# The beginning of a two-layer trunk kernel: conditioning row by rounded and low diagonals, the first modulation sum in two halves, the identity on another queue, the lower bound moved back

## The chip, the cores and the metric

The kernel runs on one core of one Trainium2 chip. The metric is device time in microseconds of one execution, as the median of several runs. Engines are named as in the profile: PE (TensorE's matmuls), PEld (its weight loads), DVE (VectorE), ACT (ScalarE), POOL (GpSimd), and SP, which here only issues transfers.

## The reference, cut to what matters

Two layers work on 512 positions of 1024 channels. The first mixes by a gated linear recurrence, the second by chunked band attention, and each has a SwiGLU feed-forward part. In front of each part stands an RMS norm whose result is scaled and shifted by a vector computed from one conditioning vector `c`:

```python
c_act = jax.nn.silu(c)
sm = jax.nn.softmax(a_lb, axis=0)
lower_bounds = jnp.cumsum(sm, axis=0) - sm[0]
...
mod = c_act @ mod_w[layer] + mod_b[layer]
sh1, sc1, g1, sh2, sc2, g2 = jnp.split(mod, N_MOD, axis=-1)
u = modulate(rms_norm(h, norm_mix[layer]), sh1, sc1)     # x * (1 + scale) + shift
# first mixer:
q, z_f, v, g = jnp.split(u @ w_in, [...], axis=-1)
f = lbf + (1 - lbf) * jax.nn.sigmoid(z_f)
```

There is one layer of the first kind, so the softmax for the lower bound runs over one element, and the bound is zero.

## The kernel before, in words

Data lie with channels on the 128 partitions: `h[j]`, j = 0 to 7, is 128 channels by 512 positions. Weights and activations are each split into a rounded high part (by ACT) and the remainder as a low part (by DVE), and a product is three matmuls: high by high, high by low, low by high (`mm3`).

*The opening.* SP issues the loads. `cols` (all the small vectors by columns) comes first, then `ident` (a 128x128 identity), then, for each j, a row block of the modulation matrix (`mrow`, 512 KB), `h[j]` (256 KB) and the first weights (`first_r`, six blocks of 128 columns, 384 KB). ACT takes the sigmoid of `c`, DVE multiplies it by `c` to get `cact`. DVE then scales the identity by one column of `cact` at a time (`dc`, L1293), and PE multiplies a matrix of ones by each of these diagonals (L1294): every partition of `crow` then holds the whole row of 1024 conditioning values. ACT and DVE copy it from PSUM to SBUF (L1306 to L1308). `KEEP` matmuls whose result is not used (L1305) keep PE at work meanwhile.

*The loop over j.* `mod_entry(j, 1)` (L952, L955) multiplies a block of the modulation matrix by `crow` on DVE and adds along the row; ACT makes the scale `a1[j]` from it. `rounded` (L974, ACT) and `rest` (L977, DVE) give the two parts of `h[j]` times that scale; `high` (L962, ACT) and `low` (L965, DVE) the two parts of the first weights; `square` (ACT) and an addition (L1322, DVE) the squares for the norm. `first_mm(j)` is 18 matmuls into six PSUM banks, the projections of heads 0 to 2 before the norm's factor and shift. When the squares of all j are added, `mean_square` (L295) and, after ACT and POOL, `bcast` (L313, L314) give the norm's factor on all partitions; the products of j = 6 stand around them, and those of j = 7 after.

*After that* the normed `u` is made, the value projection (`av`) begins, `shift_sums` on DVE and L1404 on PE give the biases `fb`, and `gates(0, None)` (L1021 to L1044) takes the sigmoids of heads 0 and 1. The lower bound enters there, as `lb` and `oml` (one minus it).

*Order.* From the loads to `push(56)` the code stands in `tc.manual_schedule()`: its instructions keep the order in which they are written, on each engine. Instructions outside that block are placed by the compiler's list scheduler, before, between or after them. The lower bound and `cact` stand outside it in the kernel before. The heads' recurrence (`core`, whose DVE lines L1059 and L1068 alternate with PE's L1078 and L1092) and the remaining projections (`filler`, advanced by `push`) follow outside the block.

Of the kernel before, what the change touches and what calls it, by code (L numbers as in the profile page):

```python
# [62 lines left out]
V1_AFTER, CREDIT, RATES = 1, 3.0, (3.5, 16, 1.375, 56, 1.5)  # L63


KEEP = 5


EARLY = (3, 5)
# [6 lines left out]
def trunk(ctx: ExitStack, tc: tile.TileContext, d, out):  # L76
# [13 lines left out]
    cols = cst.tile([P, NCOL], F32, tag="cols", name="cols")  # L90
    nc.sync.dma_start(cols, d["cols"])
    ident = cst.tile([P, P], F32, tag="ident", name="ident")
    nc.sync.dma_start(ident, d["ident"])
    h = [cst.tile([P, S], F32, tag=f"h{j}", name=f"h{j}") for j in range(KT)]

    ones = cst.tile([P, P], F32, tag="ones", name="ones")
# [9 lines left out]

    lb = cst.tile([P, AH], F32, tag="lb", name="lb")
    oml = cst.tile([P, AH], F32, tag="oml", name="oml")
    lbt = sm.tile([P, AH], F32, tag="lbt", name="lbt")
    V.tensor_sub(lbt, cols[:, C_LB:C_LB + AH], cols[:, C_LB:C_LB + AH])  # L110
    lbe = sm.tile([P, AH], F32, tag="lbe", name="lbe")
    A.activation(lbe, lbt, AF.Exp)
    lbr = sm.tile([P, AH], F32, tag="lbr", name="lbr")
    V.reciprocal(lbr, lbe)
    lbs = sm.tile([P, AH], F32, tag="lbs", name="lbs")
    V.tensor_mul(lbs, lbe, lbr)
    V.tensor_sub(lb, lbs, lbs)
    V.tensor_scalar(oml, lb, -1.0, 1.0, op0=ALU.mult, op1=ALU.add)

    cact = cst.tile([P, KT], F32, tag="cact", name="cact")  # L120
    csig = sm.tile([P, KT], F32, tag="csig", name="csig")
    A.activation(csig, cols[:, C_C:C_C + KT], AF.Sigmoid)
    V.tensor_mul(cact, cols[:, C_C:C_C + KT], csig)


    def by_transfer(key):
# [800 lines left out]
    def load_mod(j, v):  # L927

        if v and j in (0, 2):
            t = hp.tile([P, 3, D], F32, tag="kq", name=f"mrow{v}_{j}", bufs=2)  # L930
            for i, k in enumerate((j, 4 + j, 5 + j)):
                mrow[k, 1] = t[:, i, :]
        elif v and j < 4:
            mrow[j, v] = hp.tile([P, D], F32, tag="f", name=f"mrow{v}_{j}", bufs=2)
        elif not v and j in (4, 5):
            if j == 4:
                t = hp.tile([P, NB, D], F32, tag="vt", name="mrow0_4")
                mrow[4, 0], mrow[5, 0] = t[:, 0, :], t[:, 1, :]
        elif not v:
            pool, tag = ((hp, "mraw2"), (mp, "mraw"))[j in (2, 3)]  # L940
            mrow[j, v] = pool.tile([P, D], F32, tag=tag, name=f"mrow{v}_{j}", bufs=2)
        nc.sync.dma_start(mrow[j, v], d["modw"][v, j])

    def load_first(j):
        tag = ("on0", "on1", "on2", "a256", "fr4", "fr5", "fr6", "on3")[j]
        fraw[j] = hp.tile([P, 6, P], F32, tag=tag, name=f"first_r{j}")
        nc.sync.dma_start(fraw[j], d["a_first"][j])
# [12 lines left out]
    def high(j):  # L960
        wfs[j] = [wp.tile([P, 6, P], F32R, tag="w" + x, name=f"first{j}_{x}") for x in "hl"]
        A.activation(wfs[j][0], fraw[j], AF.Copy)  # L962

    def low(j):
        V.tensor_sub(wfs[j][1], fraw[j], wfs[j][0])  # L965
# [6 lines left out]
    def rounded(j):  # L972
        u[j] = [up.tile([P, S], F32R, tag=f"u{x}{j}", name=f"u00{x}{j}", bufs=1) for x in "hl"]
        A.activation(u[j][0], h[j], AF.Copy, scale=a1[j])  # L974
# [308 lines left out]
                step()  # L1283

    with tc.manual_schedule():
        dcs = hp.tile([P, KT, P], F32, tag="on3", name="dc")

        pcs = []
        for r in range(2):
            dc = dcs[:, NB * r:NB * r + NB, :]  # L1290
            pcs.append(bank(f"crow{r}"))
            for k in range(NB):
                V.tensor_scalar_mul(dc[:, k, :], ident, cact[:, NB * r + k:NB * r + k + 1])  # L1293
                T.matmul(pcs[r][:, k * P:(k + 1) * P], ones, dc[:, k, :], start=True, stop=True)  # L1294
        for j in range(KT):
            load_mod(j, 1) if (j, 1) not in mrow else nc.sync.dma_start(mrow[j, 1], d["modw"][1, j])
            nc.sync.dma_start(h[j], d["xT"][j * P:(j + 1) * P, :])
            load_first(j)
        for k in range(6):
            load_mod(k, 0)  # L1300
        load(1)
        gb = cst.tile([P, KT], F32, tag="gb", name="gb")
        V.scalar_tensor_tensor(gb, cols[:, C_MB + 8:C_MB + 16], 1.0, cols[:, C_NM:C_NM + KT], op0=ALU.add, op1=ALU.mult)
        for _ in range(KEEP):
            T.matmul(first[0][:, 0:256], ones, dcs[:, 0:2, :].rearrange("p k c -> p (k c)"), start=True, stop=True)  # L1305
        A.activation(crow[:, 0:S], pcs[0], AF.Copy)  # L1306
        A.activation(crow[:, S:S + 256], pcs[1][:, 0:256], AF.Copy)
        V.tensor_copy(crow[:, S + 256:D], pcs[1][:, 256:S])  # L1308
        high(0)
        a1.append(mod_entry(0, 1))  # L1310
        rounded(0)
        square(0)
        for j in range(KT):
            if j == 0:
                low(j)
                rest(j)
            if j + 1 < KT:
                a1.append(mod_entry(j + 1, 1))
            if j:
                rest(j)  # L1320
                low(j)
                V.tensor_add(acc, acc, sqs.pop(j))  # L1322
                if j == KT - 1:
                    pst = mean_square(acc, "n0")
                    rs = rstd(pst, "n0")
                    shs = [mod_entry(0, 0), mod_entry(1, 0)]
                    first_mm(j - 1, range(3))
                    rb = bcast(rs, "n0")
                    first_mm(j - 1, range(3, 6))
                else:  # L1330
                    first_mm(j - 1)
            if j + 1 < KT:
                rounded(j + 1)
                high(j + 1)
                square(j + 1)
        rbs = hp.tile([P, S], F32, tag="rbs", name="rbs")
        A.activation(rbs, rb, AF.Copy)
        shs.append(mod_entry(2, 0))
        ts = []

        def weighted(k):
            if k < KT:
                ts.append(normed(k, a1[k]))

        def complete(k):

            def between():
                if 1 < k < KT - 1:
                    shs.append(mod_entry(k + 1, 0))
                if k != 1:  # L1350
                    weighted(k + 1)

            shifted(k, ts[k], shs[k], between)
            if k == 1:
                weighted(2)
            if k < 2:
                load_mod(6 + k, 0)

        state["meanwhile"] = lambda: (weighted(0), complete(0))
        fetch(0, 0)  # L1360
        first_mm(KT - 1)
        early = {p: (hp.tile([P, 3, 2, S], F32, tag="kq", name=f"kq{p}", bufs=2),
                     hp.tile([P, 2, S], F32, tag="f", name=f"f{p}", bufs=2)) for p in range(2)}

        def evacuate(i):
            hd = i // 2
            A.activation(early[hd // 2][1][:, hd % 2, :] if i % 2 == 0 else early[hd // 2][0][:, 0, hd % 2, :],
                         first[i], AF.Copy)

        pa = hp.tile([P, 6, P], F32, tag="ad", name="first_pa")  # L1370

        def shift_sums(k):

            if k:
                V.scalar_tensor_tensor(pa, fraw[k], shs[k], pa, op0=ALU.mult, op1=ALU.add)
            else:
                V.tensor_scalar_mul(pa, fraw[0], shs[0])

        def renorm(i):

            hd = i // 2
            t = early[hd // 2][1][:, hd % 2, :] if i % 2 == 0 else early[hd // 2][0][:, 0, hd % 2, :]
            V.tensor_mul(t, first[i] if hd else t, rbs)

        complete(1)
        for kp in range(KT // 2):
            if kp + 1 < KT // 2:
                state["meanwhile"] = lambda: complete(2 * kp + 2)
            push(8 * kp + 1)
            if kp == 0:  # L1390
                evacuate(0)
                evacuate(1)
            if kp + 1 < KT // 2:
                complete(2 * kp + 3)
            push(8 * kp + 8)
        for k in range(KT):
            shift_sums(k)
            if k > 4:
                push(33 + 6 * (k - 5))
        for i in range(4):  # L1400
            renorm(i)
        pb = bank("first_b")
        for i in range(6):
            T.matmul(pb[:, i:i + 1], pa[:, i, :], ones[:, 0:1], start=True, stop=True)  # L1404
        fb = cst.tile([P, 2, 6], F32, tag="fb", name="fb")
        V.tensor_copy(fb[:, 0, :], pb[:, 0:6])
        state["mods_after"] = V.tensor_scalar_mul(fb[:, 1, :], pb[:, 0:6], -1.0)
        fetch(state["used"], SPLIT_AHEAD)
        gate[0] = gates(0, None)
        renorm(4)  # L1410
        renorm(5)
        u = [u[j] for j in range(KT)]
        push(56)
# [540 lines left out]
```

## Time and profile before

| | |
|---|---|
| median of 3 runs | 1214.94 us (1214.26 to 1215.57) |
| profiled execution, its own time | 1215.52 us |
| its span, first to last instruction | 1213.6 us |
| PE busy | 1199.2 us |
| DVE busy | 1008.5 us |
| ACT busy | 670.4 us |
| mean granted TensorE clock | 0.999 |

The span is 1.9 us shorter than the execution's time, because the time includes what lies before the first and behind the last instruction. A row of a timeline has the start in us from the span's start, the duration, the engine (with a q for its queue's own instructions), the source line, the operation, the tile written and those read, the shapes, the count, and in brackets the idle time of the engine before it with what ended it. A row of the chain has start, length and what was running or being waited for. In a group's row, the numbers behind the bar are busy time and the mean ns of one, and then the engine's idle time before them.

### The profile page before, as it was taken

The numbers are of one execution on the slowest core, as the hardware profiler recorded it, in microseconds if no ns is written. First come the engines' busy times: TensorE is split into PE (matmuls) and PEld (weight loads), VectorE is DVE, ScalarE is ACT, GpSimd is POOL, SyncE is SP. The second block draws the span as 40 slices with busy tenths as digits, with TensorE's granted clock in tenths as the row PEclk, the third lists the DMA queues.
The fourth block names the chain that finished last, engine by engine and source line by source line (L and its number), as shares of the span: only waits on it lengthen the run. The fifth ranks groups of instructions, "written<-read, shape, count | busy, mean of one in ns | idle before, by whom it ended". The sixth has DMA issues, their size and how long they took to land.

```text
span 1213.6 us, 22300 instructions
## 1 busy us (share of the span) xinstructions
PE 1199.2 (99%) x8758; PEld 1052.1 (87%) x8758; DVE 1008.5 (83%) x1821; ACT 670.4 (55%) x1204; POOL 51.0 (4%) x59
## 2 busy tenths in 40 slices
PE   8999999999999999999999999999999999999997
PEld 7887788788899999988888887777889999998997
DVE  8997778778989999987688878886797888977984
ACT  6455456443656666652228556674465566666553
POOL 0100000000000000000001100000100000001100
PEclk9999999999999999999999999999999999999999
DMA  9643354365423444458776987783734566546842
GB/s 356 255 128 104 106 191 141 108 204 191 121 89 125 154 140 140 138 191 280 235 238 180 251 236 201 195 251 79 214 98 157 184 202 207 171 133 153 221 125 92
DMA packets 71401, 211.94 MB, mean 175 GB/s; under 512 B 7552, under 2 KB 10240, under 8 KB 71296
## 3 DMA queue, kind: packets, MB, share of 16 engines
q1 hardware_dynamic: 63952, 194.27, 48.3%
q0 software_dynamic: 7200, 15.99, 7.8%
q8 instruction: 68, 1.11, 0.4%
q14 instruction: 37, 0.30, 0.1%
q10 hardware_dynamic: 144, 0.26, 0.1%
HBM read 204.99 MB, written 20.97 MB: 186 GB/s over the span
## 4 chain that ended last, share of the span: by engine, by line
PE 85%; DVE 7%; ACT 2%; issue 2%; DMA 2%; SPq 0%; POOL 0%; POOLq 0%; ACTq 0%; DVEq 0%
PE f_r L644 9%; PE f_r L645 9%; PE f_r L643 9%; PE f_o L244 4%; PE f_o L243 4%; PE f_o L245 4%; PE f_or L835 2%; PE f_or L834 2%; PE f_or L833 2%; PE bo L1611 1%; PE av L266 1%; PE f L245 1%; PE f L243 1%; PE bo L243 1%; PE f L244 1%
## 5 line engine op out<-in xcount | busy, mean ns | idle before, releaser
L645 PE MATMUL f_r<-f_h,f_w_l 128*128 128x256 f32 x1008 | 278.7, 276 | 0.0
L644 PE MATMUL f_r<-f_l,f_w_h 128*128 128x256 f32 x1008 | 278.7, 276 | 0.0
L643 PE MATMUL f_r<-f_h,f_w_h 128*128 128x256 f32 x1008 | 278.7, 276 | 0.0
L644 PEld LDWEIGHTS f_r<-f_l,f_w_h 128*128 128x128 f32 x1008 | 189.5, 188 | 0.1
L643 PEld LDWEIGHTS f_r<-f_h,f_w_h 128*128 128x128 f32 x1008 | 189.3, 188 | 0.1
L645 PEld LDWEIGHTS f_r<-f_h,f_w_l 128*128 128x128 f32 x1008 | 189.3, 188 | 0.0
L393 DVE SCALAR_TENSOR_TENSOR mw<-mw,crow 128x1024 f32<-128x1024 f32 x96 | 115.7, 1219 | 2.0 <-DMA mw<-in_modw 2.0
L593 ACT ACTIVATE f_w_h<-f_x 128x1024 fp32r<-128x1024 f32 x72 | 76.8, 1066 | 50.4 <-PE f_r L644 38.9
L594 DVE TENSOR_TENSOR f_w_l<-f_x,f_w_h 128x1024 fp32r<-128x1024 f32 x72 | 88.2, 1225 | 8.7 <-ACT f_w_h L593 5.2
L594 DVE TENSOR_TENSOR f_w_l<-r_f_c,f_w_h 128x1024 fp32r<-128x1024 f32 x72 | 68.8, 955 | 21.8 <-ACT f_w_h L593 21.8
L593 ACT ACTIVATE f_w_h<-r_f_c 128x1024 fp32r<-128x1024 f32 x72 | 61.1, 849 | 46.6 <-PE f_r L644 46.6
L149 ACT ACTIVATE f_o_h<-r_f_o 128x1024 fp32r<-128x1024 f32 (+2 forms) x39 | 34.3, 890 | 70.4 <-PE f_o L244 51.5
L244 PE MATMUL f_o<-f_p,f_o_h 128*128 128x512 f32 x176 | 68.6, 390 | 0.0
L245 PE MATMUL f_o<-f_p,f_o_l 128*128 128x512 f32 x176 | 68.5, 390 | 0.0
L243 PE MATMUL f_o<-f_p,f_o_h 128*128 128x512 f32 x176 | 68.3, 389 | 0.0
L1586 ACT ACTIVATE sb<-sb,st 128x128 f32<-128x128 f32 (+1 forms) x64 | 35.8, 559 | 39.3 <-DVE st L1585 39.0
L157 DVE TENSOR_TENSOR f_o_l<-r_f_o,f_o_h 128x1024 fp32r<-128x1024 f32 (+2 forms) x35 | 36.1, 1035 | 22.4 <-ACT f_o_h L149 22.1
L1068 DVE TENSOR_TENSOR kq<-kq,t 128x1024 f32<-128x1024 f32 x28 | 34.2, 1222 | 8.0 <-PE l L1135 3.3
L245 PEld LDWEIGHTS f_o<-f_p,f_o_l 128*128 128x128 f32 x176 | 33.0, 188 | 7.4 <-DVE f_o_l L157 0.5
L244 PEld LDWEIGHTS f_o<-f_p,f_o_h 128*128 128x128 f32 x176 | 33.0, 188 | 7.0 <-DVE f_p L545 0.3
L243 PEld LDWEIGHTS f_o<-f_p,f_o_h 128*128 128x128 f32 x176 | 33.0, 188 | 6.8
L245 PE MATMUL f<-f_h,f_l 128*128 128x512 f32 x96 | 36.9, 391 | 0.3 <-DMA f_l<-r_f 0.3
(517 smaller groups left out, 3213.6 us busy)
## 6 DMA issues: line engine op xcount, KB each, us to landing
mw<-in_modw SPq DMA_DIRECT2D x96, 512.0 KB, 4.5
r_f_c<-in_ffn_in SPq DMA_DIRECT2D x72, 512.0 KB, 3.4
ws<-in_ffn_in SPq DMA_DIRECT2D x18, 512.0 KB, 5.5
ws<-in_ffn_in POOLq DMA_DIRECT2D x18, 512.0 KB, 8.9
f_x<-ws SPq DMA_DIRECT2D x36, 256.0 KB, 3.0
mrow<-in_modw SPq DMA_DIRECT2D x16, 512.0 KB, 8.3
r_f<-in_ffn_in SPq DMA_DIRECT2D x16, 512.0 KB, 3.6
r_f_o<-in_ffn_out SPq DMA_DIRECT2D x16, 512.0 KB, 3.6
```

Source lines behind the costliest of these rows:

```text
L149: A.activation(wh, raw, AF.Copy)
L157: low = V.tensor_sub(wl, raw, wh)
L243: T.matmul(ps, wh[:, kt, :], uh, start=start, stop=False)
L244: T.matmul(ps, wh[:, kt, :], ul, start=False, stop=False)
L245: return T.matmul(ps, wl[:, kt, :], uh, start=False, stop=stop)
L393: V.scalar_tensor_tensor(mw, mw, 1.0, crow, op0=ALU.mult, op1=ALU.mult, accum_out=raw[:, j:j + 1])
L593: A.activation(wh, raw, AF.Copy)
L594: V.tensor_sub(wl, raw, wh)
L643: T.matmul(ps, wh[:, j, :], uh, start=f, stop=False, skip_group_check=True)
L644: T.matmul(ps, wh[:, j, :], ul, start=False, stop=False, skip_group_check=True)
L645: T.matmul(ps, wl[:, j, :], uh, start=False, stop=stop and j == 3, skip_group_check=True)
L1586: A.activation(s[:, 0:n], s[:, 0:n], AF.Exp, bias=st[:, 1:2], accum_out=st[:, 2:3])
```

## The change

- The identity's transfer is issued by ACT instead of SP.
- `cact` is one Silu on ACT instead of a sigmoid on ACT and a product on DVE.
- The lower bound's six small operations become a function, called inside the hand-ordered block between a weight's split and `gates(0, None)`.
- The diagonals are split: ACT writes the rounded diagonal (`dch`), DVE the remainder (`dcl`). PE multiplies ones by four diagonals at a time, once for the rounded and once for the low part, 512 columns each, instead of eight matmuls of 128 columns in full precision. The remainders lie in buffers that the first weights of j = 5 and 6 use later.
- Seven matmuls that only keep PE at work stand ahead of these and eight behind, each ones by ones (128 columns), instead of five of 256 columns.
- For j = 0 the modulation sum is taken in two halves straight from PSUM, each with its own scale step on ACT, and the first weights' parts in two halves. ACT copies all of `crow`.
- In the loop, a j's steps stand together: `high`, `mod_entry`, `rounded`, `square`, `low`, `rest`, addition. Before, the modulation sum of j + 1 stood ahead of `rest` and `low` of j. The products, one j behind, keep their places, and so do `mean_square` and `bcast`.
- Loads of a j come in the order `mrow`, `first_r`, `h`.

```diff
-KEEP = 5
+KEEP = (7, 8)
...
-    nc.sync.dma_start(ident, d["ident"])
+    A.dma_start(ident, d["ident"])
...
+    def lower_bound():
+        V.tensor_sub(lbt, cols[:, C_LB:C_LB + AH], cols[:, C_LB:C_LB + AH])
+        A.activation(lbe, lbt, AF.Exp)
+        V.reciprocal(lbr, lbe)
+        V.tensor_mul(lbs, lbe, lbr)
+        V.tensor_sub(lb, lbs, lbs)
+        V.tensor_scalar(oml, lb, -1.0, 1.0, op0=ALU.mult, op1=ALU.add)
...
-    A.activation(csig, cols[:, C_C:C_C + KT], AF.Sigmoid)
-    V.tensor_mul(cact, cols[:, C_C:C_C + KT], csig)
+    A.activation(cact, cols[:, C_C:C_C + KT], AF.Silu)
...
-        dcs = hp.tile([P, KT, P], F32, tag="on3", name="dc")
-
+        for _ in range(KEEP[0]):
+            T.matmul(first[0][:, 0:P], ones, ones, start=True, stop=True)
+        load_mod(0, 1)
+        load_first(0)
+        nc.sync.dma_start(h[0], d["xT"][0:P, :])
+        dhs = hp.tile([P, KT, P], F32R, tag="on3", name="dch")
+        dls = [hp.tile([P, NB, P], F32R, tag=tag, name=f"dcl_{tag}") for tag in ("fr5", "fr6")]
         pcs = []
         for r in range(2):
-            dc = dcs[:, NB * r:NB * r + NB, :]
             pcs.append(bank(f"crow{r}"))
             for k in range(NB):
-                V.tensor_scalar_mul(dc[:, k, :], ident, cact[:, NB * r + k:NB * r + k + 1])
-                T.matmul(pcs[r][:, k * P:(k + 1) * P], ones, dc[:, k, :], start=True, stop=True)
-        for j in range(KT):
+                c1 = cact[:, NB * r + k:NB * r + k + 1]
+                A.activation(dhs[:, NB * r + k, :], ident, AF.Copy, scale=c1)
+                V.scalar_tensor_tensor(dls[r][:, k, :], ident, c1, dhs[:, NB * r + k, :], op0=ALU.mult, op1=ALU.subtract)
+            for i, x in enumerate((dhs[:, NB * r:NB * r + NB, :], dls[r])):
+                T.matmul(pcs[r], ones[:, :].bitcast(F32R), x.rearrange("p k c -> p (k c)"), start=not i, stop=bool(i))
+        for j in range(1, KT):
             load_mod(j, 1) if (j, 1) not in mrow else nc.sync.dma_start(mrow[j, 1], d["modw"][1, j])
+            load_first(j)
             nc.sync.dma_start(h[j], d["xT"][j * P:(j + 1) * P, :])
-            load_first(j)
...
-        for _ in range(KEEP):
-            T.matmul(first[0][:, 0:256], ones, dcs[:, 0:2, :].rearrange("p k c -> p (k c)"), start=True, stop=True)
+        for _ in range(KEEP[1]):
+            T.matmul(first[0][:, 0:P], ones, ones, start=True, stop=True)
         A.activation(crow[:, 0:S], pcs[0], AF.Copy)
-        A.activation(crow[:, S:S + 256], pcs[1][:, 0:256], AF.Copy)
-        V.tensor_copy(crow[:, S + 256:D], pcs[1][:, 256:S])
-        high(0)
-        a1.append(mod_entry(0, 1))
+        A.activation(crow[:, S:D], pcs[1], AF.Copy)
+        wfs[0] = [wp.tile([P, 6, P], F32R, tag="w" + x, name=f"first0_{x}") for x in "hl"]
+        A.activation(wfs[0][0][:, 0:3], fraw[0][:, 0:3], AF.Copy)
+        mw, r = mrow.pop((0, 1)), [sm.tile([P, 1], F32, tag="m1", name=f"m1_0{x}", bufs=4) for x in "ab"]
+        for x in range(2):
+            c = slice(x * S, x * S + S)
+            V.scalar_tensor_tensor(mw[:, c], mw[:, c], 1.0, pcs[x], op0=ALU.mult, op1=ALU.mult, accum_out=r[x])
+        V.tensor_sub(wfs[0][1][:, 0:3], fraw[0][:, 0:3], wfs[0][0][:, 0:3])
+        g0 = sm.tile([P, 1], F32, tag="a0", name="a1_0a", bufs=KT)
+        A.activation(g0, r[0], AF.Identity, scale=cols[:, C_NM:C_NM + 1], bias=gb[:, 0:1])
+        a1.append(sm.tile([P, 1], F32, tag="a1", name="a1_0", bufs=KT))
+        A.activation(a1[0], r[1], AF.Identity, scale=cols[:, C_NM:C_NM + 1], bias=g0)
         rounded(0)
+        A.activation(wfs[0][0][:, 3:6], fraw[0][:, 3:6], AF.Copy)
         square(0)
-        for j in range(KT):
-            if j == 0:
-                low(j)
-                rest(j)
-            if j + 1 < KT:
-                a1.append(mod_entry(j + 1, 1))
-            if j:
-                rest(j)
-                low(j)
-                V.tensor_add(acc, acc, sqs.pop(j))
...
-            if j + 1 < KT:
-                rounded(j + 1)
-                high(j + 1)
-                square(j + 1)
+        rest(0)
+        V.tensor_sub(wfs[0][1][:, 3:6], fraw[0][:, 3:6], wfs[0][0][:, 3:6])
+        for j in range(1, KT):
+            high(j)
+            a1.append(mod_entry(j, 1))
+            rounded(j)
+            square(j)
+            low(j)
+            rest(j)
+            V.tensor_add(acc, acc, sqs.pop(j))
+            if j < KT - 1:
+                first_mm(j - 1)
+        pst = mean_square(acc, "n0")
+        rs = rstd(pst, "n0")
+        shs = [mod_entry(0, 0), mod_entry(1, 0)]
+        first_mm(KT - 2, range(3))
+        rb = bcast(rs, "n0")
+        first_mm(KT - 2, range(3, 6))
...
         fetch(state["used"], SPLIT_AHEAD)
+        lower_bound()
         gate[0] = gates(0, None)
```

More of the change, by code (lines that the diff above doesn't have):

```diff
@@ L108, in trunk @@
     oml = cst.tile([P, AH], F32, tag="oml", name="oml")
[L109 to L118, printed above, removed]
+    lbt, lbe, lbr, lbs = (sm.tile([P, AH], F32, tag=x, name=x) for x in ("lbt", "lbe", "lbr", "lbs"))
+    def lower_bound():
[5 more added lines that the diff above has]
+        V.tensor_scalar(oml, lb, -1.0, 1.0, op0=ALU.mult, op1=ALU.add)
     cact = cst.tile([P, KT], F32, tag="cact", name="cact")
     csig = sm.tile([P, KT], F32, tag="csig", name="csig")
-    A.activation(csig, cols[:, C_C:C_C + KT], AF.Sigmoid)
-    V.tensor_mul(cact, cols[:, C_C:C_C + KT], csig)
+    A.activation(cact, cols[:, C_C:C_C + KT], AF.Silu)
     def by_transfer(key):
@@ L1311, in trunk @@
+        V.tensor_sub(wfs[0][1][:, 0:3], fraw[0][:, 0:3], wfs[0][0][:, 0:3])
[3 more added lines that the diff above has]
+        A.activation(a1[0], r[1], AF.Identity, scale=cols[:, C_NM:C_NM + 1], bias=g0)
         rounded(0)
+        A.activation(wfs[0][0][:, 3:6], fraw[0][:, 3:6], AF.Copy)
         square(0)
-        for j in range(KT):
-            if j == 0:
-                low(j)
-                rest(j)
-            if j + 1 < KT:
-                a1.append(mod_entry(j + 1, 1))
-            if j:
-                rest(j)
-                low(j)
[L1322 to L1331, printed above, removed]
-            if j + 1 < KT:
-                rounded(j + 1)
-                high(j + 1)
-                square(j + 1)
```

## The prediction

> **What bounds the kernel now.** I read the page's busy shares first, then the chain over the opening 40 us, then the timelines of DVE and ACT over the same stretch, then the 20 us around the gates of the first head pair.
>
> ```profile
> PE 1199.2 (99%) x8758; PEld 1052.1 (87%) x8758; DVE 1008.5 (83%) x1821; ACT 670.4 (55%) x1204; POOL 51.0 (4%) x59
> ```
>
> PE is busy for 1199.2 of 1213.6 us. So time is won only by starting PE's real work sooner or by removing waits of PE, and lost by putting a wait in front of PE. The chain of the first 40 us, where the change is:
>
> ```profile
> 0.74 1.98 DMA cols<-in_cols
> 3.57 3.78 PE crow L1294 x16
> 7.35 3.37 PE first L1305 x10
> 10.73 4.42 PE first L1001 x18
> 15.15 0.23 PE first L243
> 35.86 0.78 PE n_ss L295 x8
> 38.83 0.91 PE n_rb L314 x8
> ```
>
> Real products (`first_mm`) begin at 10.73. Before that come the spreading of the conditioning row (crow) and five filling matmuls (L1305). From 10.73 PE runs products of j = 0 to 5, then at 35.86 the mean square of row tile sums (`n_ss`), then those of j = 6 and 7 with the broadcast (`n_rb`) between. Eighteen products take 4.42 us at j = 0, and the next ninety take 35.86 - 15.15 = 20.71, or 4.1 per j. What stands beside PE in that stretch is DVE, here one whole j and the last one:
>
> ```profile
> 11.38 1.22 DVE L952 SCALAR_TENSOR_TENSOR mrow<-mrow,crow 128x1024 f32<-128x1024 f32 x1
> 12.53 1.22 DVE L952 SCALAR_TENSOR_TENSOR mrow<-mrow,crow 128x1024 f32<-128x1024 f32 x1
> 13.82 0.75 DVE L977 SCALAR_TENSOR_TENSOR u00l<-h,a,u00h 128x512 fp32r<-128x512 f32 x1
> 16.03 1.22 DVE L952 SCALAR_TENSOR_TENSOR mrow<-mrow,crow 128x1024 f32<-128x1024 f32 x1
> 17.18 0.75 DVE L977 SCALAR_TENSOR_TENSOR u00l<-h,a,u00h 128x512 fp32r<-128x512 f32 x1
> 17.84 0.95 DVE L965 TENSOR_TENSOR first_l<-first_r,first_h 128x768 fp32r<-128x768 f32 x1
> 18.71 0.68 DVE L1322 TENSOR_TENSOR acc<-acc,n_sq 128x512 f32<-128x512 f32 x1
> 19.31 1.22 DVE L952 SCALAR_TENSOR_TENSOR mrow<-mrow,crow 128x1024 f32<-128x1024 f32 x1
> 33.97 0.68 DVE L1322 TENSOR_TENSOR acc<-acc,n_sq 128x512 f32<-128x512 f32 x1
> ```
>
> Columns: start, duration, engine, line, operation. DVE has no gap between 16.03 and 19.31: the modulation sum (start to next start 1.15), the low half of u (0.66), the low half of the weights (0.87), the squares' addition (0.60), together 3.28 per j. It ends the last addition at 34.65, and PE comes for it at 35.86. So DVE is 1.2 us ahead of PE there, and no more. This is the row that decides.
>
> **The change part by part.** The rows of ACT, of two groups with their mean ns (L1586, L219), and of SP's issues that I use; the last is the issue at 3.06, with its us to landing:
>
> ```profile
> 2.74 0.21 ACT L122 ACTIVATE csig<-cols 128x8 f32<-128x8 f32 x1 [0.72 <-DMA cols<-in_cols]
> 2.96 1.28 ACT L112 ACT_TABLE_LOAD   x1
> 4.26 0.21 ACT L112 ACTIVATE lbe<-lbt 128x8 f32<-128x8 f32 x1
> 5.68 0.60 ACT L1306 ACTIVATE crow<-crow 128x512 f32<-128x512 f32 x1 [1.22 <-PE crow L1294]
> 9.95 0.72 ACT L974 ACTIVATE u00h<-h,a 128x512 fp32r<-128x512 f32 x1
> 10.58 0.61 ACT L970 ACTIVATE acc<-h 128x512 f32<-128x512 f32 x1
> 17.30 0.39 ACT L955 ACTIVATE a<-m,gb,cols 128x1 f32<-128x1 f32 x1
> 17.72 0.73 ACT L974 ACTIVATE u00h<-h,a 128x512 fp32r<-128x512 f32 x1
> L1586 ACT ACTIVATE sb<-sb,st 128x128 f32<-128x128 f32 x16 | 6.4, 401 | 13.7 <-DVE st L1585 13.7
> L219 DVE SCALAR_TENSOR_TENSOR wsh_k<-r_k,mod_shk,wsh_k 128x128 f32<-128x128 f32 x14 | 4.9, 351 | 0.3
> 1.18 0.42 SPq L93 DMA_DIRECT2D ident<-in_ident  x1
> 1.64 0.43 SPq L942 DMA_DIRECT2D mrow<-in_modw  x1
> 3.06 0.43 SPq L942 DMA_DIRECT2D mrow<-in_modw  x1
> mrow<-in_modw SPq DMA_DIRECT2D x1, 512.0 KB, 6.2
> ```
>
> *Identity by ACT's queue.* Every load of SP behind it is issued one place, 0.46 us, sooner (1.18 to 1.64). ACT issues one transfer before its first table load of 1.28 us. Even with 0.4 for the issue that load ends near 2.4, before cols lands at 2.72, so it costs nothing; were that cover gone, 0.4.
>
> *Silu for sigmoid and product.* One operation of 0.21 replaces 0.21 and DVE's product: `cact` at 2.95, about 0.2 sooner.
>
> *Diagonals.* Eight ACT copies of 128x128, 0.40 each by the nearest form (L1586), 0.31 apart (ACT's next starts 0.09 before the end: 9.95, 0.72, 10.58): 2.97 to 5.54. Each has a DVE remainder of 0.35 behind it; the last ends at 5.93. Then one pass of 512 columns. A pass of 128 columns takes 3.78/16 = 0.24 here and 0.91/8 = 0.11 at 38.83: PE starts at half its later rate. A product of 512 takes 0.23 later, so 0.45 here, and 0.2 to drain: 6.6. In the old form crow's last pass ended at 7.35.
>
> *To the first product.* ACT copies crow's second half (0.60) to 7.2, three weight columns (384 elements, about 0.51 between 0.40 and 0.61) to 7.7, two scale steps of 0.39 to 8.4, rounds u (0.73) to 9.1. PE starts at 9.2 instead of 10.73: 1.5 us sooner. DVE's two half sums, 0.67 each with the reading of the sum, run beside (pcs[1] at 6.6, so done at 7.4) and are not late. The eight filling matmuls, sixteen passes, end at 6.6 + 1.8 = 8.4, or at half rate at 10.4; the latter would delay the start by 1.2, which the wait below covers.
>
> *The new order of a j.* Now DVE does modulation sum, weights' low half, u's low half, addition, all of the same j. The low half of u needs the sum's own result: ACT's scale starts 1.27 after the sum (16.03 to 17.30), the rounding 0.42 later, and the low half could start 2.44 after the sum (11.38 to 13.82, where another sum filled the time). The weights' low half fills only 0.87 of the 1.29 between. So a j takes 2.44 + 0.66 + 0.60 = 3.70 instead of 3.28. This is the wait that the change adds; behind it on DVE stands the addition, and for the last addition waits PE.
>
> *Sum of the beginning.* u's rounding ends at 9.1; then DVE does u's low half (0.66) and the weights' second half (0.47), and the sum of j = 1 starts at 10.3. That of j = 7 starts at 10.3 + 6 x 3.70 = 32.5, its addition ends 2.44 + 0.66 + 0.68 = 3.78 later, at 36.3. PE comes to it at 9.2 + 4.4 + 5 x 4.1 = 34.1 and waits 2.2 us. The mean square starts at 36.35 instead of 35.86: **+0.5**. What follows has the same order and lengths. Ends: the sum of j = 1 can't start before its row is there; issued at 3.06 and 6.2 long it landed at 9.2, one place sooner 8.8: 1.5 less, so -1.0. If copies and passes take longer by 0.7 in all, +1.2.
>
> *Lower bound later.* At the start it frees ACT of 1.28 + 0.21 and DVE of five small operations; DVE did them while crow was not ready, and ACT's would have been in the copies' way, which is why nothing is gained for it above. It now stands between the split of a value weight and the gates of heads 0 and 1 (the last row is a window: busy us and instructions of PE, PEld, DVE, ACT, POOL):
>
> ```profile
> 74.39 1.28 ACT L1021 ACT_TABLE_LOAD   x1
> 78.32 1.22 DVE L157 TENSOR_TENSOR av_l<-r_av,av_h 128x1024 fp32r<-128x1024 f32 x1
> 78.37 0.72 ACT L1021 ACTIVATE sgq<-kq,fb 128x512 f32<-128x512 f32 x1 [2.69 <-DVE fb L1406]
> 80.19 1.06 ACT L149 ACTIVATE av_h<-r_av 128x1024 fp32r<-128x1024 f32 x1 [0.48 <-ACT kq L1022]
> 81.28 1.23 DVE L157 TENSOR_TENSOR av_l<-r_av,av_h 128x1024 fp32r<-128x1024 f32 x1 [1.08 <-ACT av_h L149]
> 99.36 1.22 DVE L1068 TENSOR_TENSOR kq<-kq,t 128x1024 f32<-128x1024 f32 x1
> 101.22 0.76 PE L1092 MATMUL fine<-kq 128*32 128x32 f32 x64
> 80.00:100.00 20.00, 20.00 (x329) 15.85 (x327) 18.77 (x29) 11.79 (x17) 0.00 (x0) 1.00 0.25 80
> ```
>
> Now the sigmoid's table is loaded at 74.39, in ACT's idle time. After the change exp's table takes that place, and sigmoid's load stands behind the exp. The exp waits for DVE's difference, which is queued behind the weight's low half (78.32 + 1.14 + 0.17 = 79.63); exp to 79.87, table to 81.17, first sigmoid at 81.19 instead of 78.37. DVE's four remaining small operations (0.2 each) fall into that wait. The second weight split then ends 2.26 later, and DVE has next to no idle time up to 100 (18.77 of 20, 1.08 of the rest just spent). PE's L1092 at 101.22 has 101.22 - 100.58 = 0.64 in hand, so PE would stand 2.26 - 0.64 = 1.6 in all. That is the upper end. The lower end is 0: outside the hand-written stretch the order is the scheduler's (the split at 80.19 stands between sigmoids that precede it in the code), and it can put more value products ahead of L1092. I take **+0.6**, nearer to the low end, since part of the delay (the exp and its wait) is plain to it and the table load may not be.
>
> The Trainium skill, "ScalarE: Activation LUTs", section "What ACT_TABLE_LOAD costs", gives a switch 1283 ns and 1380 ns of drain, 2.66 us. The trace has 1.28 and exp at 4.26, right behind the load (2.96 + 1.28 = 4.24), with the operation ahead of it ended at 2.95: no drain of that size. By the page the second load would bring 1.4 us more and the sum +2.5.
>
> **Sum:** +0.5 + 0.6 = **+1.1 us**. The profiled execution took 1215.52 (span 1213.6 and 1.9 around it), 0.58 above the median of 1214.94; on the median that is **1216.0**.
>
> **The rivals.**
>
> 1. *The earlier start stays.* If the addition of j = 7 isn't late (a j of DVE still takes 3.3, because ACT answers sooner), PE keeps its 1.5, the gates cost nothing, 1213.4. For it: DVE starts its sums 2 us sooner than now. Against: the 2.44 is ACT's own two operations, which nothing shortens. 0.14.
>
> 2. *The gates cost all of it.* +0.5 + 1.6: 1217.0. For it: the dense DVE row; against: the value products that can fill. 0.12; with the upper end of the beginning 1217.7, past 0.2%.
>
> 3. *Slower, by PE's rate.* PE begins at half rate, for some 6 us: crow's passes above, then L1305's ten of 256 columns in 3.37, 0.34 on average where 0.23 is the later rate. If its new idle time of 2.2 us before the mean square is enough to put it back there, 6 us of work take 3 us more: 1216.0 + 3 = 1219.0. It decides from the gap at which the rate falls, which no row shows: PE's longest wait after its start is this one.
>
> ```profile
> PE bo L244 <- DVE ol L1629: 0.9, 1, 0.9
> ```
>
> A chance of 0.06. The Trainium skill, "TensorE: Matmul & The Clock Gate", Part 1, lets the rate fall after an idle window of about 3.4 us; by that rule 2.2 would not do, and the slow first microseconds agree with it.
>
> 4. *Identity's transfer on another queue brings nothing forward, or slows cols.* Then copies and first product stand up to 0.4 later: 1216.4, inside the main case.
>
> **How the numbers follow.** The measurement tells about 0.2%, 2.4 us, from no change. The main case has 0.68 (with rival 4), 1213.9 to 1217.6 by the bounds -1.0 to +1.2 and 0 to 1.6. Rivals 1 to 3 have 0.14, 0.12 and 0.06. From rival 1 down 0.3 for run spread comes the low end 1213.1, and 1218.2 leaves rival 3 out. Faster by over 0.2% (under 1212.5) needs rival 1 and luck in the scheduler's later order: 0.06. Slower (over 1217.4) is rival 3, half of rival 2: 0.12. The rest, 0.82, is no change.
>
> **What would show it.** In the chain: crow's end near 6.6, first product near 9.2, then a wait of PE for DVE's `acc` near 34 to 36 and the mean square at 36.3. In DVE's timeline: 3.7 per j, and an idle 0.4 before each low half of u. In ACT's: table loads at the start, at about 74 and at about 80. The prediction is wrong if the period stays 3.3, if the mean square comes before 35, if products after the wait take twice as long, or if PE waits over 2 us between 88 and 105.

## The result, and the profile after

The changed kernel takes 1223.84 us (median; 1223.72 to 1227.38) against 1214.95 for the kernel before on the same chip: 1.008 times as long, 95% interval 1.0069 to 1.0090. That is slower by 8.9 us, where 1216.0 and "no change" were predicted, and above the range. The profiled execution has a span of 1221.7 instead of 1213.6 us, and its mean granted TensorE clock is 0.996 instead of 0.999.

Most line numbers stand two lower than before, and the opening's lines are new. PE's busy time is up by only 2.7 us; the other 5.4 of the 8.1 are new idle time of PE:

```profile
PE 1201.9 (98%) x8766; PEld 1054.6 (86%) x8766; DVE 1009.4 (83%) x1822; ACT 673.4 (55%) x1214; POOL 50.8 (4%) x59
```

The chain of the first 43 us after (start, length, what ran):

```profile
3.12 2.46 ACT dch L1296 x8
5.62 0.91 PE crow L1299 x2
8.39 0.73 ACT u00h L972
35.66 0.69 DVE acc L1336
36.40 1.05 PE n_ss L293 x8
37.80 0.23 PE first L242
39.45 0.43 PE first L242
40.30 1.71 PE n_rb L312 x8
42.01 0.34 PE first L241
```

The row of conditioning is spread at 6.53, u is rounded at 9.12, and the mean square starts at 36.40, each within 0.1 of its step in the prediction. Against before that start is 0.7 later and not 0.5: the chain's 35.86 of before is where the step ahead of it ends, and the first of the eight matmuls starts at 35.70 in the timeline. PE reaches the mean square early and waits:

```profile
PE n_ss L293 <- DVE acc L1336: 2.4, 1, 2.4
```

What was not expected comes two microseconds behind the wait. The same matmul (512 columns) takes 0.23 at 37.80 and 0.43 at 39.45, and the broadcast `n_rb` 1.71 where it took 0.91. The windows after (stretch, its length, PE busy with its instructions, granted clock, DMA share, GB/s) name it:

```profile
33.00:37.00 4.00, 1.58 (x11) 1.00 1.03 410
37.00:39.00 2.00, 2.00 (x12) 0.93 0.95 336
39.00:41.00 2.00, 2.00 (x9) 0.50 0.97 342
41.00:43.00 2.00, 2.00 (x10) 0.72 0.40 160
...
109.00:111.00 2.00, 0.79 (x34) 1.00 0.04 8
111.00:113.00 2.00, 0.69 (x16) 1.00 0.00 0
113.00:115.00 2.00, 0.83 (x4) 0.70 0.52 164
115.00:117.00 2.00, 2.00 (x9) 0.50 0.66 219
```

Behind the gap the clock is at half for 3.4 us, and a second time at 114. Matching each matmul of the two traces (its start after minus its start before) gives the account: -1.56 at the first product, +0.71 at the mean square, +2.39 at 42 us, the same through 80, then +6.5 at 113 to 120, and +8.15 at the end. So 2.4 us are lost in the opening, 4.1 at the gates of the first head pair, and 1.7 later; no run takes the last part apart.

At the gates, ACT's timeline after:

```profile
76.67 1.28 ACT L113 ACT_TABLE_LOAD   x1
81.92 0.21 ACT L113 ACTIVATE lbe<-lbt 128x8 f32<-128x8 f32 x1 [3.97 <-DVE lbt L112]
82.15 1.28 ACT L1019 ACT_TABLE_LOAD   x1
83.45 0.72 ACT L1019 ACTIVATE sgq<-kq,fb 128x512 f32<-128x512 f32 x1
88.10 1.06 ACT L147 ACTIVATE av_h<-r_av 128x1024 fp32r<-128x1024 f32 x1 [0.53 <-PE av L266]
```

Exp's table takes the idle place, exp waits for DVE's difference, and the sigmoid's table stands exposed. The first sigmoid is at 83.45 instead of 78.37: 2.4 of this is the opening's, 2.7 the gates' own. On DVE after, the remainder of one more value weight has stepped in ahead of the first gated product. The product before (L1044), and the two rows after, where it is L1042:

```profile
85.51 1.23 DVE L1044 TENSOR_TENSOR kq<-kq,f 128x1024 f32<-128x1024 f32 x1
...
89.19 1.23 DVE L155 TENSOR_TENSOR av_l<-r_av,av_h 128x1024 fp32r<-128x1024 f32 x1 [0.68 <-ACT av_h L147]
91.91 1.23 DVE L1042 TENSOR_TENSOR kq<-kq,f 128x1024 f32<-128x1024 f32 x1
```

That is 6.4 late, 4.0 of it from the gates. PE first does value products instead (no idle time up to 109), and when these are used up it waits for the recurrence (waits of PE between 103 and 116 us: in total, times, longest), where before no wait of PE itself over 0.2 stood in that stretch:

```profile
PE l L1133 <- DVE kq L1066: 1.7, 1, 1.7
PE l L1120 <- DVE kq L1066: 1.4, 1, 1.4
PE l L1104 <- DVE kq L1066: 0.7, 1, 0.7
```

### The profile page after: what moved, and what is told of

It reads as the page before. It is cut to its first block, busy times and chain, and to the rows that moved or that the text cites. A ratio compares the mean times of both kernels' runs of the same rounds, so it can differ in the third digit from the quotient of the medians.

```text
span 1221.7 us, 22331 instructions
## 1 busy us (share of the span) xinstructions
PE 1201.9 (98%) x8766; PEld 1054.6 (86%) x8766; DVE 1009.4 (83%) x1822; ACT 673.4 (55%) x1214; POOL 50.8 (4%) x59
## 4 chain that ended last, share of the span: by engine, by line
PE 81%; DVE 10%; ACT 3%; DMA 3%; issue 2%; SPq 0%; POOL 0%; POOLq 0%; DVEq 0%; ACTq 0%
PE f_r L643 9%; PE f_r L642 9%; PE f_r L641 9%; PE f_o L242 4%; PE f_o L243 4%; PE f_o L241 4%; PE f L241 2%; PE f L242 2%; PE f L243 2%; PE f_or L832 2%; PE f_or L831 2%; PE f_or L833 2%; PE av L264 1%; PE av L265 1%; PE av L266 1%
```

## The experiments

Each kernel was timed against the kernel before on the same chip. The expectations stand as they were written ahead of the runs.

| kernel | median us | minus before | ratio, 95% interval |
|---|---|---|---|
| after | 1223.84 | +8.9 | 1.0080 [1.0069, 1.0090] |
| 1. after, exp on ACT replaced by a copy plus one | 1219.91 | +4.8 | 1.0037 [1.0025, 1.0050] |
| 2. before, lower bound later | 1219.76 | +4.7 | 1.0038 [1.0025, 1.0051] |
| 3. after, old order of the loop | 1219.61 | +4.5 | 1.0036 [1.0023, 1.0049] |
| 4. after, filled gap | 1222.74 | +7.7 | 1.0060 [1.0045, 1.0075] |
| 5. after, lower bound earlier | 1221.24 | +6.7 | 1.0060 [1.0046, 1.0073] |
| 6. old order, lower bound earlier | 1218.32 | +3.7 | 1.0032 [1.0021, 1.0042] |
| 7. before, lower bound later, addition on DVE | 1214.00 | -0.6 | 0.9994 [0.9985, 1.0003] |
| 8. after, lower bound at the start | 1220.15 | +5.6 | 1.0047 [1.0033, 1.0061] |
| 9. old order, addition on DVE | 1214.97 | -0.2 | 0.9998 [0.9989, 1.0007] |
| 10. after, addition on DVE | 1219.14 | +4.0 | 1.0037 [1.0025, 1.0050] |
| 11. old order, lower bound earlier, sigmoid's table early | 1215.28 | +0.1 | 1.0001 [0.9992, 1.0010] |
| 12. filled gap, addition on DVE | 1217.20 | +2.0 | 1.0017 [1.0008, 1.0026] |

**1. The changed kernel without an exponential on ACT.**

```diff
-        A.activation(lbe, lbt, AF.Exp)
+        A.activation(lbe, lbt, AF.Identity, bias=ones[:, 0:1])
```

> The changed kernel, with the exp of the lower bound (of a difference that is zero) replaced by adding one, so that ACT needs no table for it; everything else is as changed. Theory A (the loss is made in two places, about 2.4 us at the mean square and about 4 us at the gates, the latter by ACT's exp and its two table loads): the first sigmoid stands about 1.3 us sooner behind the weight split, PE's waits at L1104, L1120 and L1133 (3.7 us in all) shrink to 2 or less and the half rate behind them goes: 1219 to 1221. Rival B (the whole loss comes from the opening and is carried on): 1223.8 as before.

It gained 3.9 us on the changed kernel, but not by what it was built for. The load that went was the one that lay hidden in ACT's idle time; the sigmoid's load still ran at 84.01, and the first sigmoid came at 85.31. It stood behind the copy, and the copy waits for DVE's difference, so at this place it needs no exp to expose the load:

```profile
83.70 0.30 ACT L113 ACTIVATE lbe<-lbt,ones 128x8 f32<-128x8 f32 x1 [5.27 <-DVE lbt L112]
84.01 1.28 ACT L1019 ACT_TABLE_LOAD   x1
```

In the scheduler's new order PE nevertheless stood only for 1.3 and 0.9 us at 100 to 116 (the 0.9 at 108 for nothing that the trace shows), and the clock stayed at 1.00 there; why this order came out better is open. What it did show is the size of the half rate: in this execution the gap before the mean square was 2.4 us again, the clock stood at 0.50 from 36.6 to 43.4, and PE was 4.1 us late at 45, where the changed kernel's profiled execution was 2.4 late.

**2. Only the lower bound later, the old opening.** The six operations of the kernel before become the function, called where the changed kernel calls it.

> The kernel before, with only the lower bound's six operations moved to the place in front of the gates. Theory A: no loss in the first 75 us, then the gates come 3 to 4 us late on DVE, PE waits behind them for 2 to 4 us and runs at half rate for a time: 1219 to 1221. Rival B (the opening makes the loss): within 2.4 us of 1214.95, as I predicted for this part (+0.6, at most +1.6).

This one edit costs 4.7 us. The opening is that of before, with clock 1.00 up to 109 us; then (windows of this kernel):

```profile
109.00:111.00 2.00, 0.78 (x16) 0.71 0.00 0
111.00:113.00 2.00, 1.25 (x6) 0.50 0.75 248
```

PE's waits are 0.7, 1.4 and 1.6 us at the same three places, and PE is 3.0 us late at 104.6 and 5.0 at 113.

**3. The old order of the loop in the changed kernel.** From j = 2 on, the modulation sum of j + 1 stands ahead of `rest` and `low` of j again:

```diff
-        for j in range(1, KT):
-            high(j)
-            a1.append(mod_entry(j, 1))
...
+        for j in range(2, KT):
+            if j + 1 < KT:
+                a1.append(mod_entry(j + 1, 1))
+            rest(j)
             low(j)
-            rest(j)
             V.tensor_add(acc, acc, sqs.pop(j))
...
```

> The changed kernel, with the loop's order from j = 2 on as before (the modulation sum of j + 1 ahead of the low parts of j); j = 0 and 1 and everything else as changed. Theory A: DVE's period is 3.3 us again, the last addition ends near 33.7, PE comes to the mean square at 34.0 and waits less than 0.5 us, no half rate follows; at 45 us PE stands 4 us ahead of the changed kernel; the gates' loss stays: 1219 to 1220.5. Rival B: 1214 or less. Rival C (the order that the scheduler makes behind the hand-written stretch is the loss, whatever the start): anything, with the opening improved and the end not.

The mean square comes at 34.44, without a gap, the clock stays at 1.00 there, and PE is 1.24 us *ahead* at the first product and 0.94 from 39 through 80 us. The gates then cost what they cost in the second run (waits of 0.7, 1.4 and 1.4), and the end is 4.5 late. So the order is the whole of the opening's loss, and the two losses are separate.

**4. Filling the gap.** Twelve matmuls of ones by ones into an unused part of the bank stand ahead of the mean square:

```diff
+        for _ in range(12):
+            T.matmul(pst[:, P:2 * P], ones, ones, start=True, stop=True)
```

> The changed kernel, with twelve matmuls of ones by ones (128 columns, 2.7 us in all at full rate) on PE in front of the mean square, where it waits 2.4 us. If the idle gap is what halves PE's rate (theory A): the mean square starts about 0.3 us later than in the changed kernel, but the broadcast's eight passes take 0.9 instead of 1.7 us, the granted clock stays at 1.00 between 37 and 43 us, and 1.4 to 2 us are won: 1222. If the rate falls for another reason (rival D: the transfers or DVE's reads of the bank): it falls here too, 1224.

The filling ran from 33.90 to 36.74, the mean square started 0.2 later than after, and yet PE was only 1.36 late at 45 us, since the clock stayed at 1.00. The gates (waits of 0.7, 1.4 and 1.4, clock 0.50 at 113) then brought the whole to 7.7; run 12 has the filling without the gates' loss.

**5. The lower bound earlier in the hand-written order**, ahead of the splits and norms of the first weights instead of right before the gates.

> The changed kernel, with the lower bound's call moved up: ahead of the four norm products and the bias matmuls, where ACT is idle for 2.7 us and DVE for 1.5 us on the way to the biases, so that exp, its table and the sigmoid's table lie in front of the biases. Theory A (opening about 2.4 to 4 us, by the length of the half rate; gates about 4): the first sigmoid stands right behind the biases again, no wait of PE over 0.5 us from 45 to 120 us; only the opening's loss stays: 1217.3 to 1219. Rival C (the scheduler's order makes the loss behind the gates, whatever the lower bound's place): 1221 or more.

A miss: still 6.7 late. The exp was out of the way by 76.04, but the sigmoid's table was loaded at 82.80, behind a weight's split at 81.72, and the first sigmoid came at 84.09. Its opening has the same gap, and here the rate did not fall. A product behind the gap in this kernel (a timeline gives a matmul's whole duration, 0.39 at full clock, where the chain gives the 0.23 to the next one), and then the end of the gap and the same product in the kernel of run 10:

```profile
38.23 0.40 PE L241 MATMUL first<-u00h,first_h 128*128 128x512 f32 x1
```

```profile
36.89 1.86 PE L293 MATMUL n_ss<-mean,acc 128*128 128x1 f32 x8 [2.31 <-DVE acc L1336]
41.32 0.63 PE L241 MATMUL first<-u00h,first_h 128*128 128x512 f32 x1
```

The product takes 0.40 after a gap of 2.39 in the one and 0.63 after 2.31 in the other. Whether the rate falls is not settled by the length of the gap alone; run 10 shows by what.

**6. Old order and the lower bound earlier together.**

> The changed kernel with both mended: loop order as before from j = 2 on, and the lower bound's call ahead of the four norm products. Theory A: PE's first product at 9.4, mean square at 34.4, no half rate, gates on time: 1.2 us less than before, 1213.7 (0.999). Rival C: 1216 or more.

3.7 late, where 1.2 ahead was expected. PE is 1.4 ahead at the first product and 1.1 at 45 us; at the gates ACT shows why the earlier place is not enough:

```profile
73.24 0.21 ACT L113 ACTIVATE lbe<-lbt 128x8 f32<-128x8 f32 x1 [2.46 <-DVE lbt L112]
79.08 1.06 ACT L147 ACTIVATE av_h<-r_av 128x1024 fp32r<-128x1024 f32 x1 [4.68 <-issue]
80.16 1.28 ACT L1019 ACT_TABLE_LOAD   x1
81.46 0.72 ACT L1019 ACTIVATE sgq<-kq,fb 128x512 f32<-128x512 f32 x1
```

The engine idles for 4.68 us, but the table is loaded only behind the split, right before the operation that needs it.

**7. The second run without ACT's exponential**: the lower bound later in the kernel before, with DVE adding one to the zero difference.

```diff
-        A.activation(lbe, lbt, AF.Exp)
+        V.tensor_scalar_add(lbe, lbt, 1.0)
```

> The kernel before, with only the lower bound moved in front of the gates, and its exp (of a difference that is zero) done as an addition of one on DVE, so that ACT has nothing to do for it and the sigmoid's table is loaded in ACT's idle time as before. Theory A (ACT's exposed wait and second table load make the gates late): the first sigmoid stands where it stood before, DVE's five small operations bring 0.2 to 1 us, so 1215.0 to 1216. Rival E (any operations in front of the gates let a weight split slip in and change the order; ACT isn't the cause): 1218 or more, as with the exp on ACT (1219.8).

No loss: 1214.0 against 1219.76 with the exp on ACT. The first sigmoid is at 78.33, no table is loaded in this stretch, and no wait of PE over 0.2 is left there. Moving the five DVE operations costs nothing; the operation on ACT is the whole cost of the gates. The times of runs 5 and 6 lay in the range of their rival C (the scheduler's order makes the loss, whatever the place); it falls here and in run 8, where the gates are on time.

**8. The lower bound at the start in the changed kernel**, as the kernel before has it.

> The changed kernel with the lower bound at the start as before, outside the hand-written order. Theory A: gates on time again (4 us less than the changed kernel); the opening's loss stays or grows by up to 1.5, if exp's table load stands in the way of the rounded diagonals: 1217.3 to 1220. Rival C: 1222 or more.

The gates are on time again (PE's waits there 0.2 at most), but the exp's table now stands in the way of the new diagonal copies: first product at 11.14 instead of 9.17, mean square 38.24, then the same gap and clock 0.50 from 39 to 45. So the move of the lower bound did buy the opening about 2 us, and for the new opening the start isn't a free place for it.

**9. Both causes taken out**: old order of the loop (run 3) and the addition on DVE (run 7).

> The changed kernel with the old mixed order of the opening (from column two on, one rounded and one low diagonal a period) and the lower bound's exponential replaced by VectorE's addition of one (its argument, a difference of a row with itself, is zero), so no exponential table stands between ScalarE's copies and the first sigmoid. Theory A (two causes: TensorE's wait for the squares' accumulator at 34 to 36 us with the half rate behind it, and the exponential with the sigmoid's own table at the first gates): with both taken out what is left is the opening's earlier first product, 9.49 instead of 10.73 us; TensorE stays 1.2 us ahead at 45 us, no wait over 0.6 us at 100 to 115, time 1213.0 to 1214.0, 1.0 to 1.9 below before. Rival B (a third cause behind 220 us, where the changed kernel and the kernel with the mixed order alone each lost about a microsecond more): the lead is given back there, 1215 to 1216.

1214.97, the same as before, where 1213 to 1214 was expected. PE is ahead by 0.66 at the first product, 0.8 at 38 and 0.55 at 219: less than the 1.24 expected, since the filling matmuls ran at half rate here, to 10.35, and put off the first product. By 230 the lead is down to 0.04, and by 500 it is 0.7 again. One group on the way, of 64 matmuls, stops after 59 for nothing that the trace shows:

```profile
225.85 0.71 PE L1090 MATMUL fine<-kq 128*32 128x32 f32 x59
226.78 0.26 PE L1090 MATMUL fine<-kq 128*32 128x32 f32 x5 [0.22 <-issue]
```

Such a stop of 0.2 to 0.8 us, at 227 to 234 us, is in all eleven traces with the new opening, and in none of the three with the old one. It comes when 2390 matmuls have run (2391 in run 1), also in runs 4 and 12, whose filling adds 24 ahead of it and where it stands after 35 of the 64: it goes with the count of instructions and not with the work at this place. What the sequencer waits for stays open. The 0.7 by which PE ends ahead compares two single executions, and the one of before, with a span of 1213.6, is on the long side: the medians of all spans on this chip are 1213.2 before and 1213.0 here, as near as the times are. So the new opening is worth about 0.2 us, which the interval can't tell from nothing.

**10. Only the gates' cause taken out**: the changed kernel with the addition on DVE.

> The changed kernel with only the exponential replaced by VectorE's addition of one (the argument is zero). Theory A: only the opening's loss is left, +0.7 us of wait at the mean square and 0 to 3.3 us of half rate behind it: 1215.7 to 1219, and the first sigmoid directly behind its input with no table load between. Rival B (the exponential is only the occasion, the gates come late because the opening does): TensorE's waits of 0.7 to 1.7 us at 105 to 115 stay, 1220 or more. Rival C (the opening's delay is absorbed by VectorE's and ScalarE's slack behind it): 1215.

4.0 late by the median. Behind the gap the clock is 0.50 for 6.8 us in the profiled execution, which was the slowest of five. In every trace the changes of the clock lie whole multiples of 3.41 us apart, and where these stretches begin differs between executions. Stretches of this kind (PE busy, then granted clock) in run 10, in run 5, and in after:

```profile
33.39:36.80 3.41, 1.19 (x6) 1.00 1.03 410
36.81:40.21 3.40, 3.32 (x12) 0.50 0.81 300
40.21:43.61 3.40, 3.40 (x12) 0.50 0.59 208
...
32.32:35.73 3.41, 1.83 (x9) 1.00 1.02 408
35.73:39.14 3.41, 2.60 (x15) 1.00 0.89 347
...
35.29:38.70 3.41, 2.30 (x14) 1.00 0.99 383
```

In the fourteen traces the nine stretches at full clock in which PE was busy for 0.74 to 1.75 us were each followed by half clock, and those with 1.83 or more were not, but for one: the last row, of whose 2.30 us 0.92 are the mean square's passes of one column. The gap of run 10 lay almost whole in one stretch; the slightly longer one of run 5 was cut in two. So in these traces the fall goes with the share of a stretch in which PE works, and not with the gap's length, and the same gap can go either way.

Against the trace of before, PE goes from 1.19 late at the mean square to 4.13 late at the broadcast. The times spread over 4.0 us (1218.39 to 1222.37), twice the spread of run 9. A fall of the rate that differs between executions would do that, but 1.2 us of it lie outside the span, so this is not shown.

**11. The table placed by hand**: run 6 with one small sigmoid right behind the exp. Nothing of the computation is left out.

```diff
         A.activation(lbe, lbt, AF.Exp)
+        A.activation(csig, lbt, AF.Sigmoid)
```

> The changed kernel with the mixed order of the opening, the lower bound called ahead of the first four weight norms, and one small sigmoid (8 columns into an unused tile) directly behind the exponential, which loads the sigmoid's table while ScalarE waits anyway (it was idle for 4.7 us at 74 to 79 us in the same kernel without it, whose table load of 1.28 us then stood between the split and the first gate, first sigmoid at 81.46). Nothing is left out of the computation. Theory A: first sigmoid about 1.3 to 2 us sooner, near 79.5, waits at 105 to 113 gone or below 0.6, 1213.3 to 1215. Rival D (it is the exponential's own wait for VectorE, 2.46 us on an engine that takes its instructions in order, and not the table, that makes the gates late): first sigmoid no sooner than 81, the waits of 1.0 and 1.3 stay, 1217 to 1218.5.

3.0 us better than run 6, and no loss left against before:

```profile
73.57 0.21 ACT L113 ACTIVATE lbe<-lbt 128x8 f32<-128x8 f32 x1 [2.42 <-DVE lbt L112]
73.80 1.28 ACT L114 ACT_TABLE_LOAD   x1
75.09 0.21 ACT L114 ACTIVATE csig<-lbt 128x8 f32<-128x8 f32 x1
79.45 1.06 ACT L148 ACTIVATE av_h<-r_av 128x1024 fp32r<-128x1024 f32 x1 [3.20 <-issue]
80.42 0.71 ACT L1020 ACTIVATE sgq<-kq,fb 128x512 f32<-128x512 f32 x1
```

The load has gone into the idle time, and the sigmoid follows the split without a gap. Exp's own wait of 2.4 us is still there and costs nothing at this place, so the rival that blamed it falls for this place; it was the exposed table. PE's longest wait at 100 to 116 is 0.2.

**12. The half rate by itself**: run 10 with the filling of run 4.

> The changed kernel with twelve filling matmuls ahead of the mean square (TensorE then has no gap there) and the exponential replaced by VectorE's addition of one (the argument is zero). Nothing of the order is changed. Theory A: clock 1.00 through 45 us, TensorE 1.0 to 1.5 us late there (the wait and the filling, no half rate), no gates' loss: 1215.9 to 1217. If the half rate is what costs most in the opening, this is 1.5 to 3 us below the same kernel without the filling; if the rate plays no part (rival E: the wait alone), the two agree within 0.6 us.

1217.20, 1.9 below the same kernel with the gap, although it does 12 matmuls more. The clock is 1.00 from 33 to 47. The wait alone, without the half rate, is what stands between this and run 9: 2.2 us.

*The account by medians.* Each effect is the difference of two kernels: the exp with the sigmoid's table at the gates 4.9 (after less run 10), 4.7 (run 3 less run 9) or 5.3 (run 2 less run 7), each against its own kernel before; the half rate behind the gap 1.9 (run 10 less run 12), a little too low since the filling puts the mean square off (by 0.2 in run 4); the gap itself 2.2 (run 12 less run 9); the earlier first product -0.2 (run 9). Sum: 4.9 + 1.9 + 2.2 - 0.2 = 8.8 of 8.9. That it closes is by construction, each kernel being a step between after and before; that the gates' part is alike with three different openings is the check on it. The gates' part holds what the half rate adds there: by the traces, from 45 to 120 us, it is 2.1 in run 1 and 3.3 in run 5, where the clock stayed at 1.00, and 3.6 to 5.3 in after and runs 2, 3, 4 and 6, where it fell. No kernel here beats the one before by more than a measurement can tell.

## Why the prediction was wrong

*Bound.* PE as the bound, and waits of PE as what counts: right.

*Identity, Silu, diagonals, first product.* Right. 6.6 was forecast for the spread row and 6.53 came; 9.2 for the first product, and 9.17. The alternative that the filling matmuls run at half rate to 10.4 came up in the profiled executions of runs 9, 10 and 11 (they end at 10.35, 10.04 and 10.13, and the first product starts at 10.07, 9.79 and 9.88). So the 9.17 of after is the early end of what comes, and hitting it to 0.03 was in part luck.

*The new order of a j.* Right, within 0.02. These are DVE's rows of one j after, with the idle 0.35 before the low half of u:

```profile
17.70 1.22 DVE L950 SCALAR_TENSOR_TENSOR mrow<-mrow,crow 128x1024 f32<-128x1024 f32 x1
18.85 0.95 DVE L963 TENSOR_TENSOR first_l<-first_r,first_h 128x768 fp32r<-128x768 f32 x1
20.15 0.75 DVE L975 SCALAR_TENSOR_TENSOR u00l<-h,a,u00h 128x512 fp32r<-128x512 f32 x1 [0.35 <-ACT u00h L972]
20.82 0.69 DVE L1336 TENSOR_TENSOR acc<-acc,n_sq 128x512 f32<-128x512 f32 x1
21.42 1.22 DVE L950 SCALAR_TENSOR_TENSOR mrow<-mrow,crow 128x1024 f32<-128x1024 f32 x1
```

The period is 3.72 (3.70 forecast, 3.28 before), PE's gap 2.4 (2.2), the mean square 36.40 (36.35). The forecast took before's start from the chain, 35.86; with the timeline's 35.70 the term of +0.5 is +0.7.

*"What follows has the same order and lengths."* Here the first step failed. The lengths did not stay, since the rate fell behind the gap. This was rival 3, with 3 us and a chance of 0.06; it cost 1.7 in the profiled execution (from +0.71 to +2.39) and 1.9 by the medians. The chance leaned on the longest gap of before (0.9), which says nothing of 2.4, and on a rule. The Trainium skill, "TensorE: Matmul & The Clock Gate", Part 1, has the rate fall after an idle window of about 3.4 us, and says that this window runs freely of the kernel. The traces disagree with the first as a limit for a gap's length: the rate fell behind 2.31 us. They fit the second: 2.39 did nothing in run 5, and the stretches of run 10 are 3.41 us long and begin at another time in each execution. As a rival it should have had about an even chance, as the row was silent.

*Lower bound later.* This is the term that was mis-sized most: +0.6 forecast with an upper end of 1.6, and 4.7 to 5.3 measured. The first half of its working held. Exp's load in the idle place, exp behind DVE's difference and the exposed sigmoid's table made the first sigmoid 2.7 late where 2.82 was worked out; no drain beside the table was seen (load 82.15 to 83.43, sigmoid at 83.45), so the sum by the Trainium skill's "ScalarE: Activation LUTs", section "What ACT_TABLE_LOAD costs", which adds 1.38 us for it, does not fit this case. The step that failed is "the second weight split then ends 2.26 later ... PE would stand 1.6 in all. That is the upper end". Three things were taken as fixed that were not:

- Only one split was counted between the gates' operations. The scheduler put a second one ahead of the first gated product, and that was 4.0 late.
- The scheduler's freedom was booked as a help only, toward 0. It did put value products ahead and kept PE busy to 109 us, but these were then missing where the recurrence is slow, and PE waited three times, 3.8 us in all. A delay hidden by later work was put off, not absorbed.
- The new waits were priced by their length alone. Behind them the rate fell again, in after and in runs 2, 3, 4 and 6.

*Rivals 1 and 2.* The earlier start stayed only where the old order was kept (runs 3, 6, 9 and 11), and the gates' "all of it" was a third of the truth. "No change" at 0.82 followed from an upper end that was no bound.

## What to carry to other kernels

Ask of every new wait of the bounding engine not only how long it is, but what clock the engine comes back with: here waits of about 2 us, or three of 0.7 to 1.7 in a row, were followed by 3.4 or 6.8 us at half rate in most of the profiled executions (behind the gap of the opening in four of five), and filling matmuls that put the mean square off by 0.2 bought 1.9. The exp cost two loads here, of its own table and of the sigmoid's, and the second stood directly ahead of its user in ACT's order, although the engine had idled for 4.7 us before (run 6); a tiny sigmoid right behind the exp moved that load into idle time. Where a scheduler may fill a delay with later work, look for the place where that work will be missing before calling the delay absorbed.

## What the runs showed of the hardware that was not expected

- PE's granted clock went to 0.50 behind a gap of 2.3 to 2.4 us (2.3 us after its end in after, within 0.12 us of its end in runs 1, 8 and 10), and stayed there for 3.4 or 6.8 us. With the same gap it stayed at 1.00 in run 5. It changed in steps of 3.41 us, and fell after each stretch with PE busy for 1.75 us of it or less, and after one with 2.30 (run 10); in after, at 113.8, that was a stretch with 0.74 us of work.
- The mean granted clock of an execution already shows it: 0.998 to 0.999 in all executions of the kernel before, 0.993 to 0.996 in those of after, 0.998 to 0.999 in runs 9, 11 and 12.
- The new opening brings a stop of PE's sequencer of 0.2 to 0.8 us at 227 to 234 us, far behind anything that was changed, without a wait that the trace shows. It comes after 2390 matmuls (2391 in run 1), whatever they are.
